# A two-FFN decoder layer on one core: the down projections in pairs of chunks, k tiles 0-7 as seven block products

## The chip, the cores and the metric

The kernel runs on one core of one Trainium2 chip, alone. The metric is the device time of one execution in microseconds (us). Before the change it is 2019.5 us, the median of three runs (2019.46 to 2019.72). Profiles come from one execution of their own; times inside it count from its first instruction.

TensorE (PE) multiplies matrices and writes PSUM, VectorE (DVE) and ScalarE (ACT) work element by element, GpSimd (POOL) and SyncE (SP) here mostly issue DMAs. PEld is the loading of the stationary operand into TensorE.

## What is computed

One decoder layer on 256 tokens of width 2048, in float32: an FFN, a token mixer, an FFN, each added to 2^(1/4) times its input and followed by a LayerNorm.

```python
def _swiglu(x, w_gate, w_up, w_down):
    return (jax.nn.silu(x @ w_gate) * (x @ w_up)) @ w_down
...
        h = _layer_norm(ALPHA * h + 0.5 * _swiglu(h, ffn1_w_gate[l], ffn1_w_up[l], ffn1_w_down[l]),
                        ln1_g[l], ln1_b[l])
        mix = _mixer(h, positions, w_in[l], mla_q_norm_g[l], mla_w_uq[l], mla_kv_norm_g[l],
...
        h = _layer_norm(ALPHA * h + mix, ln2_g[l], ln2_b[l])
        h = _layer_norm(ALPHA * h + 0.5 * _swiglu(h, ffn2_w_gate[l], ffn2_w_up[l], ffn2_w_down[l]),
                        ln3_g[l], ln3_b[l])
```

The hidden width of an FFN is 5632, so `w_down` is 5632 x 2048. The mixer (two kinds of attention, branch projections and gates) is not touched by the change.

## The kernel before

**Matmuls.** Tokens stand in two halves `b` of 128. A product of activations with a weight is cut along k into tiles of 128 and along the output columns into chunks of 512. To keep float32 accuracy each operand is split into a high part (ACT casts it to float32r, L149) and the rest (DVE subtracts, L150), and `triple` (L201) issues three matmuls for each pair of tiles: high x high, high x low, low x high (L202, L203, L204). The activations are the stationary operand (128 x 128), the weights the moving one (128 x 512).

**Weight units.** Weights come in units of two k tiles: 128 x 1024 numbers, one DMA of 512 KB on SP's queue into one of 4 `raw` buffers (or an `sraw` buffer where blocks are added up). A unit is loaded, prepared (cast and split into a pair of tiles of the ring `wring`) and multiplied. `unit` and `advance` keep some units loaded and some prepared ahead, as `look` sets it; `set_ring` sets how many pairs the ring has. With `lag` the products of the second token half trail those of the first by some units. `tick` counts units, and `later(n, f)` runs `f` n units on. The tile framework sets the semaphores and, from priorities, the order on each engine within what the data allow.

**Gate and up** (`Hybrid`, L280). Chunks are taken in pairs. Of the first 8 k tiles and the two chunks it makes 2 x 2 blocks: tokens x k on the side of the activations, k x columns on that of the weights, and multiplies them in seven block products instead of eight, on sums and differences of blocks. The splits of the activations' combinations come from `Seven` (L249), those of the weights from in-place additions in `sraw` (L323). Between products stand plain units of the other k tiles. Here `look(3, 4)` holds, with a ring of 6 pairs and a lag of 1.

**The hidden activations h.** The result of gate and up has tokens in partitions; down needs k there. `turn_out` (L409) transposes 32 x 32 blocks on DVE and writes them with eight DMAs per 512 columns (four for each token half) to the DRAM tile `hT`; `get_h` (L536) reads a quad of 4 k tiles back (`hraw`, two DMAs of 256 KB on POOL's queue) and `split_h` (L541) splits it. There are 11 quads; the split ones stay in SBUF, in the 40 tiles of 4 KB per partition of the tag `act`, from which most of what is named here is taken.

**Down** (L573 to L590). The look-ahead is dropped to none, the pending work flushed, the ring cut to 4 pairs. Then come the four chunks of 512 columns one after the other, each with all 44 k tiles, through `project` (L206), with a lag of one unit, and of five from unit 14 of the last chunk on. Two PSUM banks (one for each token half) collect a chunk. In the first chunk `more` fetches and splits the quads of h.

**LayerNorm** (L436). `z` holds the input times 2^(1/4). `evac` (L462) adds half of the bank to it and takes statistics; behind the fourth chunk `apply` normalizes. The rows of `z` are loaded 12 to 18 units after the start of down, the vectors `gb` (gain and bias, spread over all partitions) 30 to 39 units after. In the first FFN `setup` (L611: masks, position angles, lambda for the mixer) runs 26 units after the start of down, on POOL, DVE and ACT.

Of the kernel before, what the change touches and what calls it, by code (L numbers as in the profile page):

```python
# [59 lines left out]
def layer_kernel(ctx: ExitStack, tc: tile.TileContext, a: dict, out: bass.AP):  # L60
# [15 lines left out]
    def act_tile(shape, dt=F32, name="act"):  # L76
        return apool.tile(shape, dt, tag="act", name=nm(name), bufs=SLOTS)
# [171 lines left out]
    class Seven:  # L249


        def __init__(self, x):
            self.x = x
            self.at_ = {}
            self.steps = [self.sums, lambda: self.pair(self.fa, 5, 6), lambda: self.pair(self.fb, 7, 3),
                          lambda: self.pair(x.raws[1], 2, 4), self.minus]

        def sums(self):
            a0, a1, c0, c1 = (self.x.raw(q, b) for q in range(2) for b in range(2))
            self.fa = act_tile([P, 2, 512], F32, "fa")  # L260
            self.fb = act_tile([P, 2, 512], F32, "fb")
            for out, in0, in1 in ((self.fa[:, 0, :], a1, c1), (self.fb[:, 0, :], a1, a0),
                                  (self.fa[:, 1, :], a0, self.fa[:, 0, :]), (self.fb[:, 1, :], c0, self.fa[:, 1, :])):
                V.tensor_tensor(out=out, in0=in0, in1=in1, op=ALU.subtract)

        def pair(self, src, p0, p1):
            hi, lo = (act_tile([P, 2, 512], F32R, "xs") for _ in range(2))
            split(hi, lo, src)
            for i, p in enumerate((p0, p1)):
                self.at_[p] = [t[:, i, :].rearrange("p (k t) -> p k t", k=4) for t in (hi, lo)]  # L270

        def minus(self):
            t = act_tile([P, 2, 512], F32R, "xs")
            hi, lo = t[:, 0, :], t[:, 1, :]
            a0 = self.x.raw(0, 0)
            S.mul(hi, a0, -1.0)
            V.scalar_tensor_tensor(out=lo, in0=a0, scalar=-1.0, in1=hi.bitcast(F32), op0=ALU.mult, op1=ALU.subtract)
            self.at_[1] = [v.rearrange("p (k t) -> p k t", k=4) for v in (hi, lo)]

    class Hybrid:  # L280
# [8 lines left out]
        def group(self, w0, w1, done):  # L289
# [82 lines left out]
            plain(1, end, True)  # L372

    def rows_to_quad(src, b, x, q, gain=None, shift=None):
        t = tr_bank()
# [60 lines left out]
    class LayerNorm:  # L436
        def __init__(self, scale, residual, g, bt, each, x=None, cols=None, at=(0, 8)):
            self.scale = scale
# [18 lines left out]
            for n in range(4):
                later(at[0] + 2 * n, lambda n=n: rows(n // 2, n % 2))
                later(at[1] + 3 * n, lambda n=n: vector(n // 2, n % 2))
# [47 lines left out]
    def ffn(n, x, wgu, wdn, residual, g, bt, each, first=None, between=None, nxt=None, cols=None):  # L507
# [24 lines left out]

        h = Acts(KF, "h")
        got = {}

# [5 lines left out]
        def split_h(q):  # L541
            raw = got.pop(q)
            for b in range(2):
                h.put(q, b, turned(raw[:, b, :]))

        seven = Seven(x)

# [17 lines left out]
        for p in range(1, KF // 4):  # L565
            if p == KF // 4 - 1:
                for q in range(3):
                    later(4 + 3 * q, lambda q=q: get_h(q))
                later(13, lambda: split_h(0))
                later(16, lambda: split_h(1))  # L570
# [8 lines left out]
        def more(j):  # L579
            if j == 0:  # L580
                get_h(3)
            if j % 2 == 0:
                if j // 2 + 4 < KF // 4:
                    get_h(j // 2 + 4)
                if j // 2 + 2 < KF // 4:
                    split_h(j // 2 + 2)
# [11 lines left out]
    def widen():  # L598
        set_ring(LAG + 5)
        lag[0] = LAG  # L600

    def dn_hook(c):
        return at_unit(14, widen) if c == 3 else None

# [446 lines left out]
```

## Time and profile before

| | |
|---|---|
| median of 3 runs | 2019.5 us |
| profiled execution: time | 2019.19 us |
| its span, first to last instruction | 2017.4 us |
| granted clock of TensorE, mean | 0.998 |
| loads of `in_dn` (down's weights) | 176 of 512 KB |
| reads `hraw<-hT` | 44 of 256 KB |

The profiled execution takes 1.8 us more than the span of its instructions. A stage is found in the profile by the tensors in its rows: down multiplies `wring` with `h`, gate and up with `x` and `xs`. The two down stages are the stretches from 459 to 700 us and from 1767 to 2007 us. A row of grouped instructions gives line, engine, operation, out<-in, shapes and count, then busy time and mean length of one in ns, then the idle time of the engine before them and what ended it.

### The profile page before, as it was taken

How to read it: one execution, taken by the hardware profiler on the slowest of the kernel's cores; microseconds unless marked ns; L12 is line 12 of the kernel's file. 1: busy time of each engine (PE TensorE's matmuls, PEld its weight loads, DVE VectorE, ACT ScalarE, POOL GpSimd, SP SyncE). 2: the span in 40 equal slices, each digit the busy share in tenths (PEclk: the TensorE clock that was granted, in tenths of full speed). 3: DMA queues.
4: the chain of work that ended last, by engine and by line, in shares of the span. 5: the costliest groups of instructions: out<-in, count | busy, mean ns of one | idle time of the engine just before them, and what ended most of it. 6: DMA issues, size and time to landing. Idle time of an engine off the chain costs nothing.

```text
span 2017.4 us, 25059 instructions
## 1 busy us (share of the span) xinstructions
PE 1999.8 (99%) x8976; PEld 1656.7 (82%) x8976; DVE 1528.2 (76%) x1792; ACT 1146.0 (57%) x1435; POOL 218.5 (11%) x407
## 2 busy tenths in 40 slices
PE   9999999999999999999999999999999999999997
PEld 8888888887888898878888888888888888888886
DVE  8999999997554676655665555699999999965455
ACT  6666666666333565554764444466666666753332
POOL 0110011022000013520001100002100100220000
PEclk9999999999999999999999999999999999999999
DMA  8676656668555667864456675656775666585553
GB/s 323 218 247 238 226 200 216 227 213 301 202 195 191 237 208 240 299 223 147 147 185 211 215 276 188 219 219 238 248 247 206 201 218 240 206 304 197 190 196 135
DMA packets 129165, 445.79 MB, mean 221 GB/s; under 512 B 18528, under 2 KB 18576, under 8 KB 129040
## 3 DMA queue, kind: packets, MB, share of 16 engines
q1 hardware_dynamic: 109296, 389.59, 54.5%
q0 software_dynamic: 19744, 54.60, 8.7%
q8 instruction: 70, 1.15, 0.2%
q14 instruction: 55, 0.45, 0.1%
HBM read 419.48 MB, written 24.64 MB: 220 GB/s over the span
## 4 chain that ended last, share of the span: by engine, by line
PE 94%; DMA 3%; DVE 1%; issue 1%; POOL 1%; ACT 1%; SPq 0%; DVEq 0%; ACTq 0%; POOLq 0%
PE mm L203 31%; PE mm L204 31%; PE mm L202 31%; DMA turned<-turn 1%; DMA turn<-blocks 1%; DMA invf<-in_inv_freq_dram 1%; PE tr L377 0%; POOL turn L414 0%; DMA sg<-in_subln_g_dram 0%; DVE wring L150 0%; DMA raw<-in_gu_dram 0%; ACT wring L149 0%; PE tr L827 0%; DMA raw<-in_wdv_dram 0%; PE tr L707 0%
## 5 line engine op out<-in xcount | busy, mean ns | idle before, releaser
L150 DVE TENSOR_TENSOR wring<-raw,wring 128x1024 fp32r<-128x1024 f32 (+1 forms) x583 | 701.4, 1207 | 401.1 <-ACT wring L149 395.4
L149 ACT CAST wring<-raw 128x1024 fp32r<-128x1024 f32 (+1 forms) x583 | 604.8, 1041 | 551.0 <-PE mm L204 457.9
L202 PE MATMUL mm<-wring,h 128*128 128x512 f32 (+2 forms) x1632 | 634.9, 389 | 0.0
L203 PE MATMUL mm<-wring,h 128*128 128x512 f32 (+2 forms) x1632 | 630.1, 386 | 1.9 <-DVE wring L150 1.8
L204 PE MATMUL mm<-wring,h 128*128 128x512 f32 (+2 forms) x1632 | 630.5, 387 | 0.0
L203 PEld LDWEIGHTS mm<-wring,h 128*128 128x128 f32 x1632 | 306.7, 188 | 63.9 <-DVE wring L150 3.7
L204 PEld LDWEIGHTS mm<-wring,h 128*128 128x128 f32 x1632 | 306.5, 188 | 62.2 <-DVE h L150 1.0
L202 PEld LDWEIGHTS mm<-wring,h 128*128 128x128 f32 x1632 | 306.7, 188 | 61.2 <-ACT h L149 1.0
L149 ACT CAST wring<-sraw 128x1024 fp32r<-128x1024 f32 x280 | 290.9, 1053 | 109.7 <-PE mm L204 78.6
L150 DVE TENSOR_TENSOR wring<-sraw,wring 128x1024 fp32r<-128x1024 f32 x280 | 335.7, 1219 | 6.3 <-ACT wring L149 3.6
L202 PE MATMUL mm<-wring,xs 128*128 128x512 f32 x560 | 218.1, 389 | 0.0
L203 PE MATMUL mm<-wring,xs 128*128 128x512 f32 x560 | 218.1, 389 | 0.0
L204 PE MATMUL mm<-wring,xs 128*128 128x512 f32 x560 | 218.1, 389 | 0.0
L323 DVE TENSOR_TENSOR sraw<-sraw,sraw 128x1024 f32<-128x1024 f32 x160 | 192.3, 1213 | 0.0
L414 POOL DMA_DIRECT2D hT<-blocks x176 | 95.6, 551 | 723.4 <-DVE blocks L412 669.4
L203 PE MATMUL mm<-wring,x 128*128 128x512 f32 x384 | 149.9, 390 | 0.5 <-DVE wring L150 0.5
L202 PE MATMUL mm<-wring,x 128*128 128x512 f32 x384 | 149.8, 390 | 0.0
L204 PE MATMUL mm<-wring,x 128*128 128x512 f32 x384 | 149.4, 389 | 0.0
L202 PEld LDWEIGHTS mm<-wring,xs 128*128 128x128 f32 x560 | 105.1, 188 | 21.8
L203 PEld LDWEIGHTS mm<-wring,xs 128*128 128x128 f32 x560 | 105.1, 188 | 21.8
L204 PEld LDWEIGHTS mm<-wring,xs 128*128 128x128 f32 x560 | 105.1, 188 | 21.7
L414 POOL DMA_DIRECT2D turn<-blocks x104 | 56.6, 552 | 304.3 <-DVE blocks L412 266.6
(235 smaller groups left out, 1607.5 us busy)
## 6 DMA issues: line engine op xcount, KB each, us to landing
raw<-in_gu_dram SPq DMA_DIRECT2D x191, 512.0 KB, 4.3
raw<-in_dn_dram SPq DMA_DIRECT2D x176, 512.0 KB, 4.2
sraw<-in_gu_dram SPq DMA_DIRECT2D x160, 512.0 KB, 5.2
raw<-in_wgm_dram SPq DMA_DIRECT2D x32, 512.0 KB, 3.2
raw<-in_wgd_dram SPq DMA_DIRECT2D x32, 512.0 KB, 3.4
raw<-in_w_out_dram SPq DMA_DIRECT2D x32, 512.0 KB, 3.2
hT<-blocks POOLq DMA_DIRECT2D x176, 64.0 KB, 2.2
hraw<-hT POOLq DMA_DIRECT2D x44, 256.0 KB, 4.1
```

The costliest lines, as they stand in the source:

```text
L149: S.copy(hi, src)
L150: V.tensor_tensor(out=lo, in0=src, in1=hi.bitcast(F32), op=ALU.subtract)
L202: PE.matmul(o, xh, wh, start=first, stop=False, skip_group_check=again)
L203: PE.matmul(o, xh, wl, start=False, stop=False, skip_group_check=again)
L204: PE.matmul(o, xl, wh, start=False, stop=last, skip_group_check=again)
L323: V.tensor_tensor(out=t, in0=t, in1=R[add[1]][s], op=ALU.add)
L414: nc.gpsimd.dma_start(to.rearrange("(g r) (i f) -> i r g f", g=4, i=4)[i], t[32 * i:32 * (i + 1), :].rearrange("r (g f) -> r g f", g=4))
```

## The change

Down takes its four chunks in two passes of two. In a pass (class `Folded`) k tiles 0 to 7 become seven block products of 4 tiles, the other 36 tiles plain units for both chunks, which are used for both token halves at once. Products 1, 5, 6 and 7 go to two PSUM banks of their own (`X`, `Z`, of the tag `tr`), and DVE adds them from there, with their sign and a half, straight into `z` (`fold`); products 2, 4 and 3 go into the chunks' own banks. X collects products 1, 6 and 7 one on top of the other, and is folded after each.

The combinations of h come from `Seven`, which now takes any two raw quads and an order of columns. Quads 0 and 1 of h serve the products alone. Quads 2 to 10 are split as the plain units reach them, and for the second pass they are read from DRAM and split once more. In the first pass each quad's four units of both chunks stand together; in the second pass that holds for five quads, and the last four quads give 8 units of the one chunk, then 8 of the other, these with the token halves apart and the lag of five.

Before down nothing is flushed any more: the look-ahead of 3 and 4 units and the ring of 6 pairs go on. The rows of `z` are loaded at 10, 12, 40 and 42 units, the vectors `gb` at 92 to 101.

```diff
     class Seven:
-        def __init__(self, x):
-            self.x = x
+        def __init__(self, raws, order=None):
+            self.raws, self.order = raws, order
...
+    class Folded:
+        def __init__(self, seven, at, k_tiles):
+            self.seven, self.at, self.k_tiles = seven, at, k_tiles
+            R = {n: [act_tile([P, 1024], F32, "sraw") for _ in range(2)] for n in ("11", "12", "22")}
+            R["21"] = R["12"]
+            self.R = R
+        def run(self, w0, w1, plain_units, places, fold, done, calls, tail=0):
+            R = self.R
+            blocks = {"11": (w0, 0), "12": (w1, 0), "21": (w0, 2), "22": (w1, 2)}
+            plan = {1: ("11", "11", None, "X"), 5: ("12", "11", "12", "Z"), 6: ("22", "11", "22", "X"),
+                    7: (None, "12", "22", "X"), 2: ("21", "21", None, (0, 0)), 4: (None, "11", "21", (0, 1)),
+                    3: (None, "22", None, (1, 0))}
+            after = {1: ((0, 0, -1.0),), 6: ((1, 0, 1.0),), 7: ((0, 1, -1.0), (1, 1, 1.0)),
+                     5: ((1, 0, 1.0), (1, 1, 1.0))}
...
+            def product(p, s):
+                load_block, src, other, key = plan[p]
...
+                def prep():
+                    t = R[src][s]
+                    if other is not None:
+                        V.tensor_tensor(out=t, in0=t, in1=R[other][s], op=ALU.add)
+                    pair = next_pair()
+                    split(*pair, t)
...
+                def now():
+                    wh, wl = st["pair"]
+                    xh, xl = self.seven.at_[p]
+                    for g in range(G):
+                        k = 2 * s + g
+                        add(key, xh[:, k, :], xl[:, k, :], wh[:, g, :], wl[:, g, :], s == 1 and g == 1)
+                    if s == 1:
+                        for n, b, sign in after.get(p, ()):
+                            fold(n, b, banks[key], sign)
...
+            order = deque((1, 5, 6, 7, 2, 4, 3))
+            for i, (n, j) in enumerate(plain_units):
+                if i in places:
+                    p = order.popleft()
+                    for s in range(2):
+                        product(p, s)
+                for fn in calls.get(i, ()):
+                    fn()
+                plain(n, j, i >= len(plain_units) - tail)
...
     class LayerNorm:
+        def fold(self, c, b, bank, sign):
+            z = self.z[b][c // 2][:, (c % 2) * 512:(c % 2) * 512 + 512]
+            V.scalar_tensor_tensor(out=z, in0=bank, scalar=sign * self.scale, in1=z, op0=ALU.mult, op1=ALU.add)
...
     def ffn(n, x, wgu, wdn, residual, g, bt, each, first=None, between=None, nxt=None, cols=None):
-        look(0, 0)
-        catch_up(0)
-        flush()
-        set_ring(4)
-        ln = LayerNorm(0.5, residual, g, bt, each, nxt, cols, (12, 30))
...
+        ln = LayerNorm(0.5, residual, g, bt, each, nxt, cols, ((10, 12, 40, 42), (92, 95, 98, 101)))
+        hs = Seven(got, turned)
+        for i, f in zip((9, 11, 12, 14, 10), hs.steps):
+            later(i, f)
         if n == 1:
             later(26, setup)
-        for c in range(4):
-            project(wdn[c], h, KF, 512, lambda b, bank, c=c: ln.evac(c, b, bank), hook=more if c == 0 else dn_hook(c))
+        down = Folded(hs, h_at, KF)
+        for p in range(2):
+            quads = list(range(2, KF // 4))
+            held = 4 * p
+            units = [(n, 2 * q + i) for q in quads[:len(quads) - held] for n in range(2) for i in range(2)]
+            units += [(n, 2 * q + i) for n in range(2) for q in quads[len(quads) - held:] for i in range(2)]
...
+            if p == 1:
+                calls.setdefault(len(units) - 8, []).append(widen)
+            down.run(wdn[2 * p], wdn[2 * p + 1], units, (6, 11, 16, 21, 26, 31, 35) if p == 0 else
+                     (1, 5, 10, 14, 19, 23, 27), lambda n, b, bank, sign, p=p: ln.fold(2 * p + n, b, bank, sign),
+                     lambda n, b, bank, p=p: ln.evac(2 * p + n, b, bank), calls, 8 * p)
+        look(0, 0)
```

More of the change, by code (lines that the diff above doesn't have):

```diff
@@ L267, in pair @@
             hi, lo = (act_tile([P, 2, 512], F32R, "xs") for _ in range(2))
-            split(hi, lo, src)
+            if self.order is None:
+                split(hi, lo, src)
+            else:
+                for i in range(2):
+                    split(*(t[:, i, :].rearrange("p (k i c) -> p k i c", k=4, i=4) for t in (hi, lo)),
+                          self.order(src[:, i, :]))
             for i, p in enumerate((p0, p1)):
@@ L274, in minus @@
             hi, lo = t[:, 0, :], t[:, 1, :]
-            a0 = self.x.raw(0, 0)
+            self.at_[1] = [v.rearrange("p (k t) -> p k t", k=4) for v in (hi, lo)]
+            a0 = self.raws[0][:, 0, :]
+            if self.order is not None:
+                t = tmp_tile([P, 512], "minus")
+                S.mul(t, a0, -1.0)
+                split(*(v.rearrange("p (k i c) -> p k i c", k=4, i=4) for v in (hi, lo)), self.order(t))
+                return
             S.mul(hi, a0, -1.0)
             V.scalar_tensor_tensor(out=lo, in0=a0, scalar=-1.0, in1=hi.bitcast(F32), op0=ALU.mult, op1=ALU.subtract)
-            self.at_[1] = [v.rearrange("p (k t) -> p k t", k=4) for v in (hi, lo)]
     class Hybrid:
@@ L542, in split_h, with h_at @@
             raw = got.pop(q)
+            hq[q] = [act_tile([P, 2, 4, P], F32R, "h") for _ in range(2)]
             for b in range(2):
-                h.put(q, b, turned(raw[:, b, :]))
-        seven = Seven(x)
+                split(*(t[:, b].rearrange("p k (i c) -> p k i c", i=4) for t in hq[q]), turned(raw[:, b, :]))
+        def h_at(which, k, b):
+            return hq[k // 4][which][:, b, k % 4, :]
+        seven = Seven(x.raws)
         def second(j):
@@ L566, in ffn @@
             if p == KF // 4 - 1:
[L567 to L570, printed above, removed]
+                for i, q in enumerate((2, 3, 0, 1)):
+                    later(3 + 3 * i, lambda q=q: get_h(q))
+                later(13, lambda: split_h(2))
+                later(16, lambda: split_h(3))
             hy.group(wgu[2 * p], wgu[2 * p + 1],
                      lambda n, b, bank, snap, op, p=p: sum_done(2 * p + n, b, bank, snap, op))
-        look(0, 0)
@@ L587, in ffn @@
+        for i, f in zip((9, 11, 12, 14, 10), hs.steps):
+            later(i, f)
         if n == 1:
             later(26, setup)
[L589 to L590 removed]
+        down = Folded(hs, h_at, KF)
[4 more added lines that the diff above has]
+            units += [(n, 2 * q + i) for n in range(2) for q in quads[len(quads) - held:] for i in range(2)]
+            calls = {}
+            for q in quads:
+                first_use = min(i for i, u in enumerate(units) if u[1] // 2 == q)
+                if (p, q) not in ((0, 2), (0, 3)):
+                    calls.setdefault(first_use, []).append(lambda q=q: split_h(q))
+                    at = first_use - 4
+                    if at >= 0:
+                        calls.setdefault(at, []).append(lambda q=q: get_h(q))
+                    elif p == 1:
+                        get_h(q)
+            if p == 1:
[3 more added lines that the diff above has]
+                     lambda n, b, bank, p=p: ln.evac(2 * p + n, b, bank), calls, 8 * p)
```

76 lines of the change are left out of this document (55 added, 21 removed).

## The prediction, made before the changed kernel ran

> **What bounds the kernel now.** I read the page's busy table first, then its chain of work that ended last, then the busy time by stage, and then single matmuls in order of time. In the table, behind a name, stand busy time, share of the span and number of instructions.
>
> ```profile
> PE 1999.8 (99%) x8976; PEld 1656.7 (82%) x8976; DVE 1528.2 (76%) x1792; ACT 1146.0 (57%) x1435; POOL 218.5 (11%) x407
> PE 94%; DMA 3%; DVE 1%; issue 1%; POOL 1%; ACT 1%; SPq 0%; DVEq 0%; ACTq 0%; POOLq 0%
> ```
>
> PE (TensorE's matmuls) is busy for 99% of the span and makes up 94% of the chain. DVE's 76% is an average, so here are the stages; each row is a stretch in us, its length, and busy time (instructions) of PE, PEld, DVE, ACT and POOL, then granted clock, DMA share and GB/s.
>
> ```profile
> 459.00:700.00 241.00, 239.11 (x1051) 196.48 (x1049) 138.56 (x165) 110.78 (x115) 14.64 (x27) 1.00 0.66 227
> 700.00:1316.00 616.00, 612.64 (x2862) 510.24 (x2861) 381.98 (x572) 337.89 (x511) 80.86 (x148) 1.00 0.61 212
> 1340.00:1767.00 427.00, 427.00 (x1886) 353.64 (x1885) 412.12 (x424) 277.55 (x325) 53.78 (x99) 1.00 0.66 230
> 1767.00:2007.00 240.00, 239.69 (x1058) 198.23 (x1056) 127.99 (x129) 98.10 (x99) 10.83 (x20) 1.00 0.58 207
> ```
>
> The first and last rows are the two down stages, the second is the mixer, the third gate and up of the second FFN. PE rests for no more than 0.3 us in either of the last two, even where DVE works 412 of 427 us. Down uses little over half of DVE (138.6 of 241). So down's length is its number of matmuls times their spacing, at a granted clock of 1.00 throughout. The spacing follows from two matmuls late in the second down stage (start, length, engine, line, operation):
>
> ```profile
> 1994.74 0.39 PE L204 MATMUL mm<-wring,h 128*128 128x512 f32 x1
> ...
> 2006.30 0.39 PE L204 MATMUL mm<-wring,h 128*128 128x512 f32 x1
> 2006.73 0.69 DVE L470 SCALAR_TENSOR_TENSOR z<-mm,z 128x512 f32<-128x512 f32 x1 [0.38 <-PE mm L204]
> ```
>
> 51 matmuls start after the first, up to and with the last: 11.56 us / 51 = **0.2267 us each** (the 0.39 is a pipelined length). The last row shows that the LayerNorm at the end starts when PE ends.
>
> The first down stage has 1.9 us of PE idle. The list of waits puts it down to DVE (us, times, longest), and it sits in three places between 485 and 502 us:
>
> ```profile
> PE mm L203 <- DVE wring L150: 2.4, 3, 1.0
> 485.04 0.39 PE L202 MATMUL mm<-wring,h 128*128 128x512 f32 x1
> 486.23 0.50 PE L203 MATMUL mm<-wring,h 128*128 128x512 f32 x1 [0.81 <-DVE wring L150]
> 486.57 0.39 PE L204 MATMUL mm<-wring,h 128*128 128x512 f32 x1
> ...
> 494.46 0.39 PE L202 MATMUL mm<-wring,h 128*128 128x512 f32 x1
> 494.90 0.50 PE L203 MATMUL mm<-wring,h 128*128 128x512 f32 x1
> 495.24 0.39 PE L204 MATMUL mm<-wring,h 128*128 128x512 f32 x1
> ...
> 500.39 0.49 PE L202 MATMUL mm<-wring,h 128*128 128x512 f32 x1
> 501.92 0.50 PE L203 MATMUL mm<-wring,h 128*128 128x512 f32 x1 [1.04 <-DVE wring L150]
> 502.26 0.40 PE L204 MATMUL mm<-wring,h 128*128 128x512 f32 x1
> ```
>
> Two steps should take 0.453 us. They take 1.53, 0.78 and 1.87: 1.08 + 0.33 + 1.42 = **2.8 us lost**. There DVE runs `setup` (masks, angles, lambda for the mixer), stands for its loads, and the split that PE needs (L150) is queued behind:
>
> ```profile
> 484.75 0.29 DVE L625 CAST posrow<-row_i 128x256 f32<-128x256 int32 x1 [3.64 <-DMA row_i<-in_pos_row_dram]
> 489.87 0.68 DVE L638 TENSOR_SCALAR ang<-invf,pos 128x32 f32<-128x32 f32 x4 [0.68 <-DMA invf<-in_inv_freq_dram]
> ```
>
> **The change, part by part.**
>
> *Matmuls removed.* Before, one pair of 512-column chunks over the 8 first k tiles takes 8 tiles x 2 chunks x 2 token halves x 3 = 96 matmuls; seven block products of 4 tiles x 3 take 84. Four pairs (two in each FFN): 48 fewer. PE's order shows it; `tr` is the bank of a product, `xs` a split combination of h, `mm` a chunk's bank. Before, past the fifth unit of the first down stage:
>
> ```order
> L204 MATMUL mm_3531<-wring_118,h_3507 128x512
> L202 MATMUL mm_3531<-wring_118,h_3506 128x512
> L203 MATMUL mm_3531<-wring_119,h_3506 128x512
> L204 MATMUL mm_3531<-wring_118,h_3507 128x512
> L202 MATMUL mm_3514<-wring_114,h_3502 128x512
> L203 MATMUL mm_3514<-wring_115,h_3502 128x512
> ```
>
> And in the changed kernel at the same distance from the stage's start:
>
> ```order
> L204 MATMUL tr_3659<-wring_104,xs_3580 128x512
> L202 MATMUL tr_3659<-wring_102,xs_3580 128x512
> L203 MATMUL tr_3659<-wring_103,xs_3580 128x512
> L204 MATMUL tr_3659<-wring_102,xs_3580 128x512
> L202 MATMUL tr_3659<-wring_102,xs_3580 128x512
> L203 MATMUL tr_3659<-wring_103,xs_3580 128x512
> L204 MATMUL tr_3659<-wring_102,xs_3580 128x512
> L202 MATMUL mm_3564<-wring_120,h_3312 128x512
> ```
>
> A weight pair now feeds 6 matmuls where it is a product's, and still 12 elsewhere; shape and type are the old ones. 48 x 0.2267 = **-10.88 us**, all on the path.
>
> [...]
>
> *Depth of the ring of split weights.* Down used to run with nothing looked ahead and 4 pairs of `wring`; now the gate/up look-ahead and its 6 pairs go on. DVE's order around `setup` before (rows of L150 into wring are the splits):
>
> ```order
> L150 TENSOR_TENSOR wring_121<-raw_3670,wring_120 128x1024
> L150 TENSOR_TENSOR h_3750<-hraw_3702,h_3749 128x512
> L619 CAST pos_4011<-pos_i_4009 128x2
> L621 TENSOR_SCALAR npos_4013<-pos_4011 128x2
> L150 TENSOR_TENSOR h_3825<-hraw_3742,h_3824 128x512
> L150 TENSOR_TENSOR wring_119<-raw_3686,wring_118 128x1024
> L150 TENSOR_TENSOR h_3829<-hraw_3742,h_3828 128x512
> L625 CAST posrow_4017<-row_i_4015 128x256
> L150 TENSOR_TENSOR wring_117<-raw_3709,wring_116 128x1024
> ```
>
> And now (L434 adds two weight blocks for a product):
>
> ```order
> L434 TENSOR_TENSOR sraw_3398<-sraw_3398,sraw_3400 128x1024
> L746 CAST pos_3880<-pos_i_3878 128x2
> L752 CAST posrow_3886<-row_i_3884 128x256
> L748 TENSOR_SCALAR npos_3882<-pos_3880 128x2
> L150 TENSOR_TENSOR h_3797<-hraw_3706,h_3796 128x512
> L150 TENSOR_TENSOR wring_121<-sraw_3398,wring_120 128x1024
> L150 TENSOR_TENSOR wring_119<-raw_3683,wring_118 128x1024
> L150 TENSOR_TENSOR h_3797<-hraw_3706,h_3796 128x512
> L150 TENSOR_TENSOR wring_117<-raw_3709,wring_116 128x1024
> L434 TENSOR_TENSOR sraw_3397<-sraw_3397,sraw_3401 128x1024
> L150 TENSOR_TENSOR wring_115<-raw_3726,wring_114 128x1024
> ```
>
> The even number beside each (120, 118, ...) names the pair: before they come round after 4, now after 6 (104 and 102 too). A cast into a pair waits for the pair's last matmul, so between that matmul and the next that needs the pair lie 4 half units of 6 = 24 matmuls before, and now 3 plain units and one product's two, 48, or 60 without a product: 10.9 us against 5.4. The cast and the split of one unit take from that:
>
> ```profile
> L149 ACT CAST wring<-raw 128x1024 fp32r<-128x1024 f32 x93 | 97.7, 1053 | 126.5 <-PE mm L204 112.3 <-DMA raw<-in_dn_dram 10.4 <-DMA raw<-in_wc_dram 2.5
> L150 DVE TENSOR_TENSOR wring<-raw,wring 128x1024 fp32r<-128x1024 f32 x92 | 112.4, 1223 | 94.7 <-ACT wring L149 94.5
> ```
>
> Cover for a DVE that stands still rises from 5.4 - 1.05 - 1.22 = 3.1 to 8.6 us, 5.5 more, and the longest single loss was 1.42. The four broadcast loads of norm vectors that shared the queue with `setup` also move to the stage's end. Bounds of this term: nothing gained (0) to all gained; I take all, **-2.8 us**, since both reasons point there.
>
> *DVE and ACT work added* per FFN: 12 more units to cast and split, 16 adds, 12 folds, 14 more halves of h to split, 11 instructions for the combinations. Durations:
>
> ```profile
> L323 DVE TENSOR_TENSOR sraw<-sraw,sraw 128x1024 f32<-128x1024 f32 x160 | 192.3, 1213 | 0.0
> L150 DVE TENSOR_TENSOR h<-hraw,h 128x512 fp32r<-128x512 f32 x44 | 28.7, 683 | 0.0
> L470 DVE SCALAR_TENSOR_TENSOR z<-mm,z 128x512 f32<-128x512 f32 x16 | 11.0, 688 | 11.7 <-PE mm L204 11.7
> L149 ACT CAST h<-hraw 128x512 fp32r<-128x512 f32 x6 | 3.5, 614 | 0.0
> ```
>
> 12 x 1.22 + 16 x 1.21 + 12 x 0.69 + 25 x 0.68 = 59 us: DVE goes from 138.6 to some 198 of the stage's 233. ACT gains 12 x 1.05 + 22 x 0.61 = 26 us, to 137. Both lie beside PE, and the gate/up row above shows PE unbroken with DVE at 97%. It is not even, though: the first pass of FFN 1 also holds `setup`, whose 16 groups of rows on DVE run from the first to the last of these:
>
> ```profile
> L648 DVE SCALAR_TENSOR_TENSOR ang<-turns,ang 128x128 f32<-128x128 f32 x12 | 3.5, 290 | 0.3
> L630 DVE SCALAR_TENSOR_TENSOR bias<-dist,mask 128x384 f32<-128x384 f32 x4 | 2.0, 553 | 0.0
> ...
> L663 DVE TENSOR_SCALAR lam<-ld 128x1 f32<-128x1 f32 x1 | 0.1, 146 | 0.0
> ```
>
> Together they are 10.4 us busy. That pass: 50 splits 61.2, adds 9.7, folds, evacuations and statistics 14 x 0.69 = 9.7, h 9.6, combinations 7.5, `setup` 10.4 = 108 us of DVE, against 36 x 12 + 14 x 6 = 516 matmuls = 117 us of PE. That fits, with 9 us of room. Cost taken **0**; rival two has the other bound.
>
> *New waits.* A fold waits on DVE for its product's last matmul; queued behind it are splits that PE needs no sooner than the ring's 48 matmuls later. A later product into the same bank comes at least 4 plain units (10.9 us) after the fold. **0**; without that cover each of 24 folds would cost its 0.69, 17 us.
>
> *h read again.* POOL's order at the end of the second FFN's down, before:
>
> ```order
> L539 DMA hraw_13644<-hT_9983 128x512 x2
> L451 DMA z_13428<-res_101 128x1024
> L539 DMA hraw_13684<-hT_9983 128x512 x2
> L451 DMA z_13430<-res_101 128x1024
> L451 DMA z_13429<-res_101 128x1024
> L451 DMA z_13431<-res_101 128x1024
> L456 DMA gb_13432<-in_ln_g_dram 128x1024
> ```
>
> And now:
>
> ```order
> L564 DMA z_14153<-res_101 128x1024
> L564 DMA z_14179<-res_101 128x1024
> L655 DMA hraw_14295<-hT_10097 128x512 x2
> L655 DMA hraw_14304<-hT_10097 128x512 x2
> L655 DMA hraw_14399<-hT_10097 128x512 x2
> L655 DMA hraw_14502<-hT_10097 128x512 x2
> L655 DMA hraw_14597<-hT_10097 128x512 x2
> L655 DMA hraw_14689<-hT_10097 128x512 x2
> L655 DMA hraw_14725<-hT_10097 128x512 x2
> L655 DMA hraw_14786<-hT_10097 128x512 x2
> L655 DMA hraw_14827<-hT_10097 128x512 x2
> L569 DMA gb_14972<-in_ln_g_dram 128x1024
> ```
>
> Those nine reads (`hraw`) are the second pass's own; 36 more issues in all over both FFNs. What one takes (issue on POOL, min/median/max in ns, then landing in us):
>
> ```profile
> L539 POOL DMA_DIRECT2D hraw<-hT x44: 546/546/572, 100.6 to 1778.4; - x44
> DMA to landing us min/median/max: 2.6/4.1/7.2
> ```
>
> A read waits for the tile of an earlier quad of h; two issues of 0.55 and the longest landing make 8.3 us. A quad lasts 4 plain units, 10.9 us, and a ninth of the 14 product units of 1.36, 2.1: 13.0 us, and each read is issued a quad ahead of its split. Cost **0**. The traffic grows by 36 x 256 KB = 9.4 MB, where the DMA share is 0.66 and 0.58.
>
> *Turn from gate/up to down, and end.* The last matmul on x and the first on h stand at the usual distance:
>
> ```profile
> 458.97 0.39 PE L204 MATMUL mm<-wring,x 128*128 128x512 f32 x1
> 459.20 0.39 PE L202 MATMUL mm<-wring,h 128*128 128x512 f32 x1
> ```
>
> So dropping the flush there gives nothing. Evacuation and LayerNorm behind the last matmul keep their instructions and the lag of five half units: 0.
>
> **Sum.** Profiled execution 2019.19 us - 10.88 - 2.83 = 2005.5. The median of the runs shown is 2019.5, 0.3 above it, so I forecast 2005.7 against that median.
>
> **Rivals.**
>
> *One: the stall stays.* If `setup`, now among adds and combinations, still lets PE run dry as before, 2.8 us come back: **2008.5**. For it: its loads still stand in POOL's queue behind reads of h. Against: the cover of 8.6 us. Chance 0.15.
>
> *Two: DVE becomes the bound in the first pass of FFN 1.* Combinations and `setup` (17.9 us) stand in its first half. Half of the rest is 45.1; with the old waits for loads, 3.64 + 0.68, DVE needs 67.3 us where PE needs 58.5: 8.8 too many, against a cover of 8.6. That leaves nothing if the cover is full at the start. If it is half full, since DVE comes out of a stage where it is 97% busy, PE loses 8.8 - 4.3 = 4.5: **2010.2**. Against: splits in a row overlap, as here, so 50 of them take less than 61.2:
>
> ```profile
> 502.93 2.36 DVE L150 TENSOR_TENSOR wring<-raw,wring 128x1024 fp32r<-128x1024 f32 x2 [1.06 <-ACT wring L149]
> ```
>
> FFN 2 has no `setup` and so has room. Chance 0.12.
>
> *Three: h comes late, and the change is slower.* If the tile for a read came free only when DVE has split the quad just before, DVE would stand for the round trip. DVE's room per quad is 13.0 - 108 / 9 = 1.0 us; beyond that PE waits. To give back 13.7 us and 4 more (0.2%) over 36 quads, 0.5 us each suffice, so it decides from 1.5 us of standing. At 2 us the price is 36 x 1.0 = 36 us: **2042**. For it: in-order DVE, a 40-slot tile pool that is nearly full. Against: the reads stand a quad ahead in POOL's order. Chance 0.04.
>
> *Four: the matmuls go but something unnamed takes most of it back*, within 0.2% of before (about what a measurement of this kernel tells from no change): 0.03. That the change does not do what it says is ruled out by PE's order.
>
> **How the numbers follow.** Forecast 2005.7 with 0.66; rivals 0.15, 0.12, 0.04 and 0.03. The range starts at 2004.2: the mixer has 616.0 - 612.6 = 3.4 us of PE idle, and its buffers are laid out anew, so up to half of that might go. It ends at 2010.5, just past rival two: with rival one that leaves out less than 2 in 10. Faster: 0.66 + 0.15 + 0.12 = 0.93; same 0.03; slower 0.04.
>
> **What will show it.** Right: the two down stages 5.4 us shorter by matmuls, the first 2.8 more, spacing still 0.227, no PE wait on L150 between 460 and 520 us, DVE near 200 us in each. Rival one: the same three waits. Rival two: many short PE waits on L150 in the first 100 us of FFN 1's down alone. Rival three: DVE idle before the h split, released by `hraw<-hT`. I would be wrong altogether if matmuls into a product's bank were spaced wider than 0.2267.

## The result, and the profile after

| | before | changed |
|---|---|---|
| median of 6 runs each, side by side (us) | 2019.61 | 2007.33 |
| lowest to highest | 2018.65 to 2021.70 | 2003.77 to 2009.52 |
| profiled execution: time / span | 2019.19 / 2017.4 | 2005.43 / 2003.7 |
| ratio, 95% interval | | 0.9936 [0.9923, 0.9948] |

The change saves 0.64%. The profiled execution saves 13.76 us, where the sum said 13.71; the median saves 12.3 and stands 1.6 above the forecast of 2005.7. Two runs of the experiments below, one of `stream_plain` (4115.13 us) and one of the kernel before beside it (2732.03 us), were in a slow state and are left out of ratios and means.

The page of the changed kernel, busy table and the chain of work that ended last:

```profile
PE 1987.9 (99%) x8928; PEld 1646.3 (82%) x8928; DVE 1629.5 (81%) x1922; ACT 1191.2 (59%) x1503; POOL 238.7 (12%) x443
...
PE 91%; DMA 4%; DVE 1%; issue 1%; ACT 1%; POOL 1%; SPq 0%; DVEq 0%; ACTq 0%; POOLq 0%
```

PE has 48 instructions less (8976 to 8928) and 11.9 us less of busy time; DVE has 101 us more and still makes up 1% of the chain. The two down stages, cut into their passes (stretch, length, busy time of PE, PEld, DVE, ACT and POOL, granted clock, DMA share, GB/s):

```profile
458.98:575.90 116.92, 116.92 (x517) 96.84 (x516) 103.19 (x143) 76.12 (x95) 20.67 (x38) 1.00 0.80 282
575.90:691.60 115.70, 115.57 (x510) 95.38 (x510) 86.12 (x92) 61.30 (x65) 7.05 (x13) 1.00 0.70 230
1760.00:1876.00 116.00, 116.00 (x513) 96.06 (x512) 95.33 (x105) 70.07 (x85) 17.98 (x33) 1.00 0.80 276
1876.00:1992.60 116.60, 116.60 (x517) 96.50 (x515) 83.69 (x92) 53.33 (x57) 6.51 (x12) 1.00 0.57 188
```

PE's busy time equals the length in three of the four passes and misses it by 0.13 in the second. So the stall around `setup` is gone, and nothing took its place. DVE still stands idle there, though, if for another load. DVE in order of time in that place (start, length, in brackets the idle time ahead of the row and what ended it):

```profile
480.33 1.23 DVE L434 TENSOR_TENSOR sraw<-sraw,sraw 128x1024 f32<-128x1024 f32 x1 [4.42 <-DMA sraw<-in_dn_dram]
481.48 1.22 DVE L150 TENSOR_TENSOR wring<-raw,wring 128x1024 fp32r<-128x1024 f32 x1
...
487.82 0.16 DVE L746 CAST pos<-pos_i 128x2 f32<-128x2 int32 x1
487.89 0.29 DVE L752 CAST posrow<-row_i 128x256 f32<-128x256 int32 x1
```

The rows of `setup` (L746, L752) no longer wait for their loads. But DVE stood 4.42 us for a block of weights just before, longer than the 3.64 us for `row_i` in the kernel before, and PE's windows row for this place reads

```profile
478.00:500.00 22.00, 22.00 (x98) 18.20 (x97) 19.41 (x25) 15.14 (x20) 1.63 (x3) 1.00 0.84 295
```

Not one of the 22 us is lost. The DVE groups of the first down stage that the prediction priced (count, busy, mean ns, idle ahead and its releaser):

```profile
L150 DVE TENSOR_TENSOR wring<-raw,wring 128x1024 fp32r<-128x1024 f32 x74 | 89.7, 1220 | 29.2 <-ACT wring L149 28.8
L150 DVE TENSOR_TENSOR wring<-sraw,wring 128x1024 fp32r<-128x1024 f32 x28 | 33.9, 1218 | 1.0 <-ACT wring L149 0.3
L150 DVE TENSOR_TENSOR h<-hraw,h 128x512 fp32r<-128x512 f32 x32 | 21.5, 685 | 5.9 <-ACT h L149 5.9
L434 DVE TENSOR_TENSOR sraw<-sraw,sraw 128x1024 f32<-128x1024 f32 x16 | 19.4, 1220 | 6.5 <-DMA sraw<-in_dn_dram 6.5
L577 DVE SCALAR_TENSOR_TENSOR z<-tr,z 128x512 f32<-128x512 f32 x12 | 7.9, 682 | 0.0
```

The 12 folds wait for nothing (last row, idle 0.0). And the spacing of matmuls late in the second down stage:

```profile
1981.24 0.39 PE L202 MATMUL mm<-wring,h 128*128 128x512 f32 x1
...
1992.58 0.39 PE L204 MATMUL mm<-wring,h 128*128 128x512 f32 x1
```

11.34 us for 50 steps, 0.2268 us each: as before.

**Lengths of the stages.** For all kernels below two lengths are read from the order of time: the first down stage, from the first matmul on `h` to the first transpose of its LayerNorm, and FFN 2, from the first transpose of the mixer's LayerNorm to the last matmul. Before they are 241.28 and 697.09 us, in the changed kernel 232.63 and 691.79: 8.65 and 5.30 us less, 13.95 together. The end behind the last matmul stays (11.11 and 11.08 us), and so does the turn into down.

### The profile page after: what moved, and what is told of

Read it like the earlier page. It is cut to its first block, busy times and chain, and to the rows that moved or that the text cites. A ratio compares the mean times of both kernels' runs of the same rounds, so it can differ in the third digit from the quotient of the medians.

```text
span 2003.7 us, 25261 instructions
## 1 busy us (share of the span) xinstructions
PE 1987.9 (99%) x8928; PEld 1646.3 (82%) x8928; DVE 1629.5 (81%) x1922; ACT 1191.2 (59%) x1503; POOL 238.7 (12%) x443
## 4 chain that ended last, share of the span: by engine, by line
PE 91%; DMA 4%; DVE 1%; issue 1%; ACT 1%; POOL 1%; SPq 0%; DVEq 0%; ACTq 0%; POOLq 0%
PE mm L204 29%; PE mm L202 29%; PE mm L203 29%; DMA turn<-blocks 2%; DMA turned<-turn 1%; PE tr L202 1%; PE tr L203 1%; PE tr L204 1%; POOL turn L527 1%; DVE wring L150 1%; ACT wring L149 1%; DMA raw<-in_wdq_dram 1%; PE tr L490 0%; DMA raw<-in_wdk_dram 0%; DMA raw<-in_gu_dram 0%
## 5 line engine op out<-in xcount | busy, mean ns | idle before, releaser
L150 DVE TENSOR_TENSOR wring<-raw,wring 128x1024 fp32r<-128x1024 f32 (+2 forms) x551 | 660.8, 1205 | 263.3 <-ACT wring L149 257.1
L149 ACT CAST wring<-raw 128x1024 fp32r<-128x1024 f32 (+2 forms) x551 | 570.0, 1040 | 417.6 <-PE mm L204 322.3
L202 PE MATMUL mm<-wring,h 128*128 128x512 f32 (+2 forms) x1504 | 584.5, 389 | 0.0
L204 PE MATMUL mm<-wring,h 128*128 128x512 f32 (+2 forms) x1504 | 580.1, 386 | 0.0
L203 PE MATMUL mm<-wring,h 128*128 128x512 f32 (+2 forms) x1504 | 579.2, 385 | 0.0
L149 ACT CAST wring<-sraw 128x1024 fp32r<-128x1024 f32 x336 | 349.8, 1053 | 147.9 <-PE mm L204 93.3
L150 DVE TENSOR_TENSOR wring<-sraw,wring 128x1024 fp32r<-128x1024 f32 x336 | 403.4, 1218 | 9.6 <-ACT wring L149 5.0
L204 PEld LDWEIGHTS mm<-wring,h 128*128 128x128 f32 x1504 | 282.4, 188 | 57.5 <-DVE h L150 1.0
L202 PEld LDWEIGHTS mm<-wring,h 128*128 128x128 f32 x1504 | 282.6, 188 | 56.0 <-ACT h L149 1.0
L203 PEld LDWEIGHTS mm<-wring,h 128*128 128x128 f32 x1504 | 282.6, 188 | 55.6 <-DVE wring L150 0.2
L202 PE MATMUL mm<-wring,xs 128*128 128x512 f32 x608 | 236.5, 389 | 0.0
L203 PE MATMUL mm<-wring,xs 128*128 128x512 f32 x608 | 236.5, 389 | 0.0
L204 PE MATMUL mm<-wring,xs 128*128 128x512 f32 x608 | 236.5, 389 | 0.0
L203 PEld LDWEIGHTS mm<-wring,xs 128*128 128x128 f32 x608 | 114.1, 188 | 23.7
L202 PEld LDWEIGHTS mm<-wring,xs 128*128 128x128 f32 x608 | 114.1, 188 | 23.7
L204 PEld LDWEIGHTS mm<-wring,xs 128*128 128x128 f32 x608 | 114.1, 188 | 23.7
```

The source lines that it names most:

```text
L149: S.copy(hi, src)
L150: V.tensor_tensor(out=lo, in0=src, in1=hi.bitcast(F32), op=ALU.subtract)
L202: PE.matmul(o, xh, wh, start=first, stop=False, skip_group_check=again)
L203: PE.matmul(o, xh, wl, start=False, stop=False, skip_group_check=again)
L204: PE.matmul(o, xl, wh, start=False, stop=last, skip_group_check=again)
```

## The experiments

Ten kernels were run, each with a profile and timed in three rounds beside the kernel before; a ratio is to the kernel before, with its 95% interval in brackets. A stand is time in which an engine is idle until a load or another engine is done. Two theories stood against each other. **Cover:** what counts is the lead, the matmuls between the last one on a pair of split weights and the next need of that pair; it must be longer than any stand of DVE or ACT. **Something else:** the norm-vector loads, the dropped look-ahead, the work on DVE, or the reads of h.

### Taking the products away, and taking the old ring back

`stream_plain`: streamed pairs and 6 pairs of `wring`, but all 44 k tiles plain.

```diff
-            quads = list(range(2, KF // 4))
+            quads = [2, 3, 0, 1] + list(range(4, KF // 4))
...
-            down.run(wdn[2 * p], wdn[2 * p + 1], units, (6, 11, 16, 21, 26, 31, 35) if p == 0 else
-                     (1, 5, 10, 14, 19, 23, 27), lambda n, b, bank, sign, p=p: ln.fold(2 * p + n, b, bank, sign),
+            down.run(wdn[2 * p], wdn[2 * p + 1], units, (), lambda n, b, bank, sign, p=p: ln.fold(2 * p + n, b, bank, sign),
```

> The changed kernel without its products: all 44 k tiles as plain units, streamed in two passes with the look-ahead and the ring of 6 pairs, h read again. 48 matmuls come back. Theory (10.9 us from the matmuls, 2.8 us from the stall that the deeper ring and the later norm loads remove): about 2016.7 us, 2.8 below the kernel before, first down stage (first matmul on h to the first LayerNorm transpose) 238.5 us instead of 241.3. Rival (all of the gain is from matmuls, the removed stall was chance): 2019.5 us, 241.3 us.

Measured: 2015.78 us, ratio 0.9986 [0.9976, 0.9995]; first down stage 238.07, FFN 2 697.09. So the way from before to after falls into two parts in the first down stage: 241.28 - 238.07 = 3.2 us for the stall, 238.07 - 232.63 = 5.44 us for 24 matmuls of 0.2267. In FFN 2 there is no stall to lose, and 697.09 - 691.79 = 5.3 us are the other 24 matmuls' (24 x 0.2267 = 5.44).

`products_ring4`: products as in the change, but the old turn into down.

```diff
+        look(0, 0)
+        catch_up(0)
+        flush()
+        set_ring(4)
-        ln = LayerNorm(0.5, residual, g, bt, each, nxt, cols, ((10, 12, 40, 42), (92, 95, 98, 101)))
+        ln = LayerNorm(0.5, residual, g, bt, each, nxt, cols, ((3, 5, 33, 35), (85, 88, 91, 94)))
```

(What is to run some units on moves 7 units forward with it, since nothing is ahead any more.)

> The changed kernel with the old turn: nothing looked ahead, flush, a ring of 4 pairs, delayed work moved 7 units forward so that it stands at the same places. Theory (the ring's cover of 8.6 us is what hides DVE): the stall around setup comes back with 2.8 us or more, since DVE now has more to do there; first down stage 235.5 us or more against 232.6, second longer by 0 to 3 us; total 2008.5 to 2013. Rival (the cover is not needed, the norm loads alone caused the stall): first stage 232.6, no change.

Measured: 2024.95 us, ratio 1.0028 [1.0017, 1.0038], slower than before; first stage 238.75, FFN 2 699.76. The direction was right, the size too small: FFN 2, which has no `setup`, loses 8.0 us as well, and I had given it 0 to 3. The stages are from the fastest of this kernel's eight runs, 5.3 us under their median, so they tell too little of the loss. PE in order of time at the worst place, and ACT at the one like it in FFN 2:

```profile
477.27 0.39 PE L203 MATMUL mm<-wring,h 128*128 128x512 f32 x1
480.72 0.50 PE L202 MATMUL tr<-wring,xs 128*128 128x512 f32 x1 [3.06 <-ACT wring L149]
```

```profile
1784.44 1.06 ACT L565 ACTIVATE z<-z 128x1024 f32<-128x1024 f32 x1 [4.00 <-DMA z<-res]
1785.40 1.03 ACT L149 CAST wring<-sraw 128x1024 fp32r<-128x1024 f32 x1
```

ACT, in order, stood 4.00 us for a row of `z`, and the cast for the first product was queued behind. But this kernel undid two things at once, the ring and the look-ahead, so it left open which of them costs.

### The ring by itself, in four doses

`after_ring4_keep` takes only two pairs from the ring and keeps units loaded ahead; `after_ring5_keep` takes one (with `look(3, 3)` and `set_ring(5)`).

```diff
+        look(3, 2)
+        set_ring(4)
         ln = LayerNorm(0.5, residual, g, bt, each, nxt, cols, ((10, 12, 40, 42), (92, 95, 98, 101)))
```

> The changed kernel, only the ring of split pairs cut from 6 to 4 at the start of down (with 2 instead of 4 units prepared ahead); three units stay loaded ahead and nothing is flushed. It parts the two things that products_ring4 undid together (down stages 238.75 and 699.76 us there, against 232.63 and 691.79 in the changed kernel). Lead from the last matmul on a pair to the next need of it, counted in the order: 25 to 37 matmuls as in products_ring4, so 25 x 0.2267 - 2.28 = 3.4 us of cover. Theory A, the flush with its dropped loads made most of that loss (ACT stood for z while the DMA share was 1.0): first down stage 233 to 235.5 (a stand of 4.4 us for sraw and one of 3.6 for setup against 3.4 of cover cost about 1 us), FFN 2 within 1 us of 691.8, total 2006 to 2010. Theory B, the ring's length alone makes it: 238 to 239.5 and 699 to 701, total 2018 to 2026.

Measured: 2018.68 us, ratio 1.0002 [0.9991, 1.0013]; first stage 238.99, FFN 2 696.82. Theory A fell, and B holds for the first stage and the total: with four pairs the change is worth nothing, 11.35 us of its 12.3 are gone, and the stages name the same sum (6.36 + 5.03). For FFN 2, B gave 699 to 701, 2 to 4 us too much, and the median stays 6.3 us under that of `products_ring4`; so the flush and the dropped loads cost something too. DVE and PE at the largest gap of FFN 1, and ACT at the place where FFN 2 loses most:

```profile
527.38 1.22 DVE L150 TENSOR_TENSOR wring<-raw,wring 128x1024 fp32r<-128x1024 f32 x1
531.61 2.36 DVE L434 TENSOR_TENSOR sraw<-sraw,sraw 128x1024 f32<-128x1024 f32 x2 [3.01 <-DMA sraw<-in_dn_dram]
533.89 1.22 DVE L150 TENSOR_TENSOR wring<-raw,wring 128x1024 fp32r<-128x1024 f32 x1
```

```profile
532.30 0.39 PE L202 MATMUL mm<-wring,h 128*128 128x512 f32 x1
535.16 0.79 PE L203 MATMUL mm<-wring,h 128*128 128x512 f32 x1 [2.47 <-DVE wring L150]
```

```profile
1851.92 0.62 ACT L149 CAST h<-hraw 128x512 fp32r<-128x512 f32 x1 [5.24 <-DMA hraw<-hT]
1853.41 0.62 ACT L149 CAST h<-hraw 128x512 fp32r<-128x512 f32 x1 [0.87 <-DMA hraw<-hT]
```

In the first place DVE stands for a weight block, then does two additions, and PE waits for the split behind them. In the second a late read of h holds ACT up, and the casts of weights stand behind it; PE has two gaps there of 1.44 and 1.03 us. These are stands of the kind that the changed kernel has too (4.42 us for a weight block above, 5.95 us for h below) without a loss.

> The changed kernel with the ring cut from 6 to 5 pairs for down (3 units prepared ahead), nothing flushed. Lead in the order 37 matmuls at products (4 pairs: 25 and up, 6 pairs: 49 and up), so a cover of 37 x 0.2267 - 2.28 = 6.1 us. Theory, a loss is what a single stand exceeds the cover by: with 4 pairs (cover 3.4) the longest PE gap was 2.6 us, 6.0 of stand in all, which 6.1 just covers: first down stage 232.6 to 233.6 (4 pairs: 238.99, 6 pairs: 232.63), FFN 2 691.7 to 692.7, total 2005 to 2009. Rival, the loss falls evenly with each pair: 235.8 and 694.3, total 2011 to 2014.

Measured: 2007.56 us, ratio 0.9941 [0.9927, 0.9956]; first stage 232.62, FFN 2 691.70. One pair more brings all of it back (from 238.99 and 696.82 us), and the sixth brings nothing (232.63 and 691.79): a step, not a slope.

The same number raised in the kernel before, alone:

```diff
-        set_ring(4)
+        set_ring(6)
```

> The kernel before with the one number of the ring in down raised from 4 to 6 pairs, nothing else: the part of the change that the prediction priced at 2.8 us, alone. Lead in the order 49 matmuls instead of 25, cover 8.8 us instead of 3.4. Theory, the stands of 3.6 and 0.7 us around setup are then covered: first down stage 241.28 - 3.1 = 238.2, FFN 2 unchanged at 697.1, total 2014 to 2018. Rival, without units prepared ahead (none are, in this kernel) a longer ring stays empty and the stall is back: 240 to 241.3, total 2017 to 2021.

Measured: 2016.68 us, ratio 0.9987 [0.9978, 0.9997]; first stage 238.07, FFN 2 697.15. The stall goes and DVE's stand for a load of `setup` stays, as DVE's row and PE's stretch show:

```profile
481.88 0.17 DVE L619 CAST pos<-pos_i 128x2 f32<-128x2 int32 x1 [3.64 <-DMA pos_i<-in_pos_col_dram]
```

```profile
478.00:504.00 26.00, 26.00 (x117) 21.52 (x116) 19.01 (x49) 18.52 (x23) 3.73 (x7) 1.00 0.80 261
```

That stand was not the stall's only source. Ahead of the last of its three places (1.42 of the 2.8 us lost) ACT in the kernel before stood for a block of weights and then ran its own part of `setup` before the next cast; in `before_ring6` this second stand is gone:

```profile
495.32 1.05 ACT L149 CAST wring<-raw 128x1024 fp32r<-128x1024 f32 x1 [5.17 <-DMA raw<-in_dn_dram]
```

And `stream_plain` with four pairs (the two added lines of `after_ring4_keep`):

> stream_plain (no products, all 44 k tiles plain, same output) with the ring cut to 4 pairs in the same way. Lead 37 matmuls in the order, so cover 37 x 0.2267 - 2.28 = 6.1 us, where before had 25 and stream_plain 61. Theory A, the cover decides and 6.1 us are enough for setup's stands of 3.6 us: first down stage 238.1 as in stream_plain, total 2014 to 2018. Theory B, the number of pairs decides, whatever the lead: the stall around setup is back, 240 to 241.3, total 2016.5 to 2020.

Measured: 2015.74 us, ratio 0.998 [0.9971, 0.999]; first stage 238.06, FFN 2 697.10. So four pairs alone don't make the loss. They were enough here, where each pair feeds 12 matmuls in a row, and not where a product's feeds 6. But the stands were shorter here too. DVE waits less for `setup`'s load than in the kernel before (3.64 us):

```profile
476.21 0.29 DVE L751 CAST posrow<-row_i 128x256 f32<-128x256 int32 x1 [1.52 <-DMA row_i<-in_pos_row_dram]
```

All kernels side by side:

| kernel | pairs | common least lead, matmuls | cover, us | first down stage | FFN 2 |
|---|---|---|---|---|---|
| before | 4 | 25 | 3.4 | 241.28 | 697.09 |
| `stream_ring4` | 4 | 37 | 6.1 | 238.06 | 697.10 |
| `before_ring6` | 6 | 49 | 8.8 | 238.07 | 697.15 |
| `stream_plain` | 6 | 61 | 11.5 | 238.07 | 697.09 |
| `after_ring4_keep` | 4 | 25 | 3.4 | 238.99 | 696.82 |
| `after_ring5_keep` | 5 | 37 | 6.1 | 232.62 | 691.70 |
| changed | 6 | 49 | 8.8 | 232.63 | 691.79 |

The lead is counted in the instructions' order (a few pairs have less, around the turn); cover is lead x 0.2267 less 2.28 for cast and split (1053 and 1223 ns in the first down stage before). Stands of 3.0 to 5.2 us stand in the rows of the kernels with 3.4, and they lose. FFN 2 of the kernel before loses nothing at 3.4: it has no `setup`, and its longest stand for a load is 2.4 us. That 6.1 us are enough holds for what those two kernels met: their longest stands for a load are 3.13 us (`after_ring5_keep`) and 2.50 us (`stream_ring4`) in the two down stages. That 8.8 us cover more is seen directly: 5.68 us for weights in `before_ring6` and 5.95 us for h in the changed kernel, without a loss.

How much of the cover was used can be worked out from the traces: it is the cover less the shortest time between the end of a split on DVE and the matmul that reads it. In the first down stage that time is 0.37 us in the changed kernel, 1.63 in `after_ring5_keep`, 1.08 in `before_ring6` and 2.63 in `stream_ring4`; matmuls that wait have 0.05. So `before_ring6` used 8.8 - 1.1 = 7.7 us, though the longest single stand around `setup` is 3.64: stands and the work queued between them add up, which the theory of the single stand left out. `stream_ring4` used 6.1 - 2.6 = 3.5, hardly more than 3.4, so whether its longer lead or its shorter stands saved it stays open. What the ring does by itself is shown by before and `before_ring6`, which differ in nothing else, and by `after_ring4_keep` and `after_ring5_keep`, which differ in one pair and the one unit prepared ahead that goes with it.

### The norm vectors

The prediction gave a second reason for the end of the stall: the four broadcast loads leave the queue that `setup` uses. Two kernels move these loads alone.

```diff
-                later(at[1] + 3 * n, lambda n=n: vector(n // 2, n % 2))
+                later((at[1] if at[1] != 30 else 72) + 3 * n, lambda n=n: vector(n // 2, n % 2))
```

> The kernel before, with the four broadcast loads of the norm vectors 42 units later. Theory (the ring removed the stall): it stays, first down stage 241.3 us, time within 0.5 us of before. Rival (these loads slowed setup's loads): the stall goes, 238.5 us, 2.8 us faster.

Measured: 2019.65 us, ratio 0.9998 [0.9988, 1.0007]; first stage 241.32: the stall stays.

```diff
-        ln = LayerNorm(0.5, residual, g, bt, each, nxt, cols, ((10, 12, 40, 42), (92, 95, 98, 101)))
+        ln = LayerNorm(0.5, residual, g, bt, each, nxt, cols, ((10, 12, 40, 42), (37, 40, 43, 46)))
```

> The changed kernel with the norm vectors loaded at 37 to 46 units, as early as before. Theory (cover of the ring): first down stage stays 232.6 us within 0.3. Rival (moving these loads removed the stall): 1 to 3 us longer.

Measured: 2007.84 us, ratio 0.9946 [0.9931, 0.9961]; first stage 232.62. The norm vectors have no part in it.

### The prices of rivals two and three

`after_more_dve` adds an addition for each product unit:

```diff
+                    V.tensor_tensor(out=extra, in0=t, in1=t, op=ALU.add)
                     pair = next_pair()
```

> The changed kernel with one more DVE addition of 128x1024 (1.22 us, its result unused) for each of the 14 units of products in a pass: 17 us more in each pass, 120.3 of DVE in the first pass of FFN 1 against 116.9 of PE, 112.4 of 116.0 in FFN 2. Theory, the cover is full at the start of down: in the first half of that pass DVE needs 17.9 + 51.2 + 4.4 of standing = 73.5 us where PE needs 58.5; 15.0 too many less 8.6 of cover = 6.4 us lost: first down stage 239, FFN 2 691.8 to 693, total 2012 to 2015. Rival two's assumption, cover half full: 10.7 lost, 243.3. If DVE's waits and work overlap better than the sum says: under 236.

Measured: 2013.36 us, ratio 0.9974 [0.9964, 0.9985]; first stage 239.69, FFN 2 691.75. The sum with a full cover gave 239, that with rival two's half-full one 243.3. That 239 was met so nearly is in part luck: the sum put the loss into the first half of the pass, and most of it lies in the second. Its first pass in two halves, and PE where it runs dry (its lines stand one or two further on):

```profile
458.85:517.00 58.15, 57.30 (x253) 47.14 (x252) 53.40 (x71) 36.77 (x48) 11.46 (x22) 1.00 0.73 239
517.00:576.00 59.00, 55.52 (x236) 44.52 (x235) 54.80 (x75) 34.66 (x41) 8.10 (x15) 0.97 0.85 290
```

```profile
526.64 0.50 PE L204 MATMUL tr<-wring,xs 128*128 128x512 f32 x1 [0.98 <-DVE wring L151]
...
529.05 0.49 PE L203 MATMUL tr<-wring,xs 128*128 128x512 f32 x1 [0.99 <-ACT wring L150]
530.58 0.50 PE L204 MATMUL tr<-wring,xs 128*128 128x512 f32 x1 [1.04 <-DVE wring L151]
```

DVE is busy for over 90% of either half, and PE has three waits of 1 us in a row, all for DVE or what hangs on it. So rival two's mechanism is real and starts within 17 us of added work in the first pass of FFN 1; the same 17 us cost nothing in FFN 2.

`after_h_no_lead` reads each quad of h right ahead of its split in program order:

```diff
-                    calls.setdefault(first_use, []).append(lambda q=q: split_h(q))
-                    at = first_use - 4
...
+                    calls.setdefault(first_use, []).append(lambda q=q: get_h(q))
+                    calls.setdefault(first_use, []).append(lambda q=q: split_h(q))
```

> The changed kernel with each quad of h read right ahead of its split in program order, not a quad earlier: the mechanism of rival three, to get its price. Theory, DVE in order stands for the round trip: some 6 us (two issues of 0.55 on POOL, 4.7 to land) a quad, against DVE's room of 1.5, 3.3, 2.3 and 3.7 us per quad in the four passes as measured; over 7, 9, 7 and 9 quads 85 us after 8.6 us of cover in each FFN: first down stage 255 to 285, total 2045 to 2095. Rival: a split stands 7 units (19 us) ahead of its first matmul, and DVE is ahead of PE, so a read without a lead is hidden as well: first down stage 232.6 to 234, total 2005 to 2010.

Measured: 2006.94 us, ratio 0.9942 [0.9926, 0.9958]; first stage 232.62, FFN 2 691.66. My theory was wrong by the whole 85 us. POOL in order of time tells the reason, first in the changed kernel, then in this one:

```profile
539.56 1.09 POOL L655 DMA_DIRECT2D hraw<-hT  x2 [16.46 <-DVE h L150]
547.41 1.09 POOL L655 DMA_DIRECT2D hraw<-hT  x2 [6.76 <-DVE h L150]
555.77 1.09 POOL L655 DMA_DIRECT2D hraw<-hT  x2 [7.28 <-DVE h L150]
```

```profile
535.50 1.08 POOL L655 DMA_DIRECT2D hraw<-hT  x2 [12.29 <-PE mm L204]
545.51 1.08 POOL L655 DMA_DIRECT2D hraw<-hT  x2 [8.93 <-DVE h L150]
554.16 1.09 POOL L655 DMA_DIRECT2D hraw<-hT  x2 [7.57 <-DVE h L150]
```

The reads start 1.6 to 4.1 us earlier, though they stand a quad later in the program. Their place there doesn't set them; the tile does, and that comes free, in most of these rows, when DVE has split an earlier quad. In the three rows of the changed kernel it is the quad just before: this is rival three's condition, and it holds there. It shows on ACT there, and DVE's next splits of weights come late; PE's row is the first matmul that reads the first of the three splits:

```profile
544.21 0.62 ACT L149 CAST h<-hraw 128x512 fp32r<-128x512 f32 x1 [5.95 <-DMA hraw<-hT]
547.37 3.50 DVE L150 TENSOR_TENSOR wring<-raw,wring 128x1024 fp32r<-128x1024 f32 x3 [0.26 <-ACT wring L149]
548.97 0.39 PE L203 MATMUL mm<-wring,h 128*128 128x512 f32 x1
```

ACT stood 5.95 us for h, and PE lost nothing within that pass. It was close: the first split ended at 548.60, 0.37 us before its matmul, so nearly all of the 8.8 us was used. With a cover of 3.4 a stand of this kind does cost (1851.92 in `after_ring4_keep`, above).

## Why the prediction was right, point by point

- **Matmuls removed, -10.88:** right. 5.44 us in the first down stage and 5.3 in FFN 2, at a spacing of 0.2268; the order of banks adds nothing. The traces have 226.7 ns before and 226.8 after the change, and the first stage bears that out (5.44 us / 24 = 226.7 ns).
- **Depth of the ring, -2.8:** right in sign, in the main in cause, and nearly in size: the ring alone takes 3.2 us (`before_ring6`). Of its two reasons one was wrong: the norm vectors have no effect. The stall's origin was told too narrowly, as DVE's stand for `setup`'s loads: ahead of half of the 2.8 us ACT had stood for weights, too (5.17 us, shown with `before_ring6`). And the ring was priced as a term of its own, with 0 as the worst case. Together with the products it is worth 11.4 us, since products that feed 6 matmuls a pair shorten the lead (at four pairs from 37 to 25): with four pairs most of what the products save is lost again (238.99 + 696.82 us against 241.28 + 697.09: 2.6 less instead of 10.9, so 8 us of loss where the bound given was 0).
- **DVE and ACT work, 0:** right. DVE is at 189.3 us (103.2 + 86.1) in the first down stage, forecast 198 (9 too many), and at 103.2 of 116.9 in the first pass, forecast 108 of 117. The room was real but thin: 17 us more and it is used up (7.1 us lost in `after_more_dve`).
- **New waits, 0:** right. The folds wait for nothing (idle 0.0 ahead of the 12 of the first down stage).
- **h read again, 0:** right in size, wrong in reason. The reads don't go out a quad ahead by their place in POOL's order, but when DVE frees a tile. They come late enough to hold ACT for 5.95 us, and the ring hides that, with 0.37 us to spare.
- **Turn and end, 0:** right, as the tail of 11.1 us and the passes' unbroken PE show.
- **The sum:** 2005.5 for the profiled execution, 2005.43 measured. So close a hit is luck: the profiled executions of the three other kernels with the same stages took 2005.31 to 2007.66 us, the stages fell by 13.95 us where the sum had 13.71, and part of that was lost elsewhere. The median is 1.6 us above the forecast. Taken over the 18 runs of the four kernels whose stages have the changed kernel's length, the mean is 2007.2, and over the 57 runs of the kernel before that stand beside the experiments 2019.3: 12.2 us apart, where the stages give 13.95. Some 1.8 us are thus given back elsewhere. Between the two stages lies the mixer, whose length is 606.4 to 611.3 us in the five profiles without products and 608.9 to 610.9 in the seven with them. The two overlap, so where the 1.8 us lie stays open.
- **Rivals:** one's stall did not stay, two did not reach its point, three's condition held but stayed under the cover.

## What to carry to other kernels

Before work is made cheaper for the bound engine, count what a prepared buffer now buys in its instructions: fewer matmuls per pair shorten the lead (here 6 instead of 12 took it from 37 to 25 at four pairs), and the ring may have to grow in the same edit. Size such a ring by the stands of the engines that fill it (here single ones of 3 to 6 us for weight, h or position loads) and by the work queued between them, not by their busy share alone. Where the cover was enough, one more buffer brought nothing in time here (232.62 us with five pairs, 232.63 with six), but the traces show how little was left (0.37 to 2.63 us). A wait that costs nothing may be covered rather than absent (as ACT's 5.95 us for h were here), so look for what covers it before taking the cover away.

## What the runs showed of the hardware

In `products_ring4` the granted clock fell after one long gap of PE and not after another. Two matmuls in a row start 3.45 us apart in FFN 1 and 3.7 us apart in FFN 2. Its windows, each gap and then the stretch after it (granted clock third from the end):

```profile
477.20:480.70 3.50, 0.46 (x3) 0.04 (x1) 0.32 (x2) 2.03 (x3) 0.00 (x0) 1.00 0.95 364
480.70:484.40 3.70, 3.68 (x9) 2.91 (x10) 3.70 (x6) 2.90 (x4) 0.00 (x0) 0.55 1.04 363
1782.70:1786.40 3.70, 0.44 (x2) 0.01 (x1) 0.00 (x0) 1.96 (x3) 0.55 (x1) 1.00 1.02 396
1786.40:1790.00 3.60, 3.52 (x15) 2.66 (x15) 3.54 (x4) 3.60 (x6) 0.00 (x0) 1.00 1.03 402
```

After the shorter gap the clock reads 0.55 over 3.7 us, after the longer one 1.00 over 3.6 us: 9 matmuls against 15, by estimate 6 x 0.2267 = some 1.4 us on top of the gap. It also reads 0.50 over 3.04 us after a gap of 2.86 us in `after_ring4_keep` and, in `after_more_dve`, 0.50 over 3.00 us after the three waits of 1 us shown above (last row):

```profile
532.30:535.16 2.86, 0.39 (x3) 0.00 (x1) 2.86 (x4) 2.33 (x3) 0.00 (x0) 0.94 0.02 10
535.16:538.20 3.04, 3.04 (x7) 2.46 (x8) 3.04 (x4) 0.00 (x0) 0.00 (x0) 0.50 0.53 172
...
531.50:534.50 3.00, 2.53 (x7) 1.51 (x6) 3.00 (x5) 1.48 (x2) 1.09 (x2) 0.50 0.73 218
```

Whole runs differ, too: the eight of `products_ring4` go from 2019.67 us at a mean granted clock of 0.997 (the profiled one) to 2027.42 us at 0.995 and 2027.15 us at 0.994, while all six of the changed kernel have 0.997 to 0.999. What decides whether the clock falls after a gap, none of these runs shows.
